# In-chunk products over all 128 rows with a zero-padded X, and a smaller descriptor ring for GpSimd

## The chip, the core and the metric

The kernel runs on one NeuronCore of a Trainium2 chip. Its engines are named as in the profile: PE (TensorE, the matrix engine; PEld is its loading of weights), DVE (VectorE), ACT (ScalarE), POOL (GpSimd) and SP (SyncE, which here only issues DMAs). The metric is device time in microseconds (us) of one execution.

## The reference

One layer of a flow-matching backbone is applied to 128 context tokens and 512 latent tokens, all of width 2048. Each layer is a mixer and a SwiGLU. The mixer splits one projection of the normed, modulated input into a bidirectional RWKV-7 scan (16 heads of 64) and a chunked gated MLP (8 groups of 128). The part that matters here is the scan, run forward and backward for each head:

```
def _delta_scan(r, w, k, v, aa, bb, s0, reverse):
    def step(S, inp):
        r_t, w_t, k_t, v_t, a_t, b_t = inp
        sa = jnp.einsum('bhvk,bhk->bhv', S, a_t)
        S = S * w_t[:, :, None, :] + sa[..., None] * b_t[:, :, None, :] + v_t[..., None] * k_t[:, :, None, :]
        return S, jnp.einsum('bhvk,bhk->bhv', S, r_t)
    s_fin, ys = lax.scan(step, s0, xs, reverse=reverse)

p = h @ lp['w_in']
o_a, s_fin = _rwkv7_bidir(shift_fn(p[..., :C_SHIFT], lp['mu_shift']), s0, lp)
o_b = _chunk_gmlp(jax.nn.gelu(p[..., C_SHIFT:]), lp)
x = x + g1 * (jnp.concatenate([o_a, o_b], axis=-1) @ lp['w_out'])
h = _rmsnorm(x, lp['norm2_g']) * (1.0 + sc2) + sh2
ff = (jax.nn.silu(h @ lp['w_ffn_gate']) * (h @ lp['w_ffn_up'])) @ lp['w_ffn_down']
```

All data are float32. Outputs are the two token streams after the last norm and the final context states of the scan.

## The kernel before, in words

Channels lie on the 128 partitions (rows) and the 640 tokens on the free axis, so a block of 128 channels holds a pair of heads: head 0 in rows 0 to 64, head 1 in rows 64 to 128. The kernel runs in five stages: modulation and norm (until about 190 us of the profile), the projection `w_in` with the preparation of the scan and the gated MLP (190 to 1200), the recurrence over chunks with half of `w_out` (to about 1560), the gate and up products, and the down product.

**The wide products of the second stage.** `win` (lines 179 to 189) multiplies blocks of `w_in` by the normed input. Both operands are split in a rounded part and a remainder (`hi`, `lo`), so a product of 128 rows by 320 tokens is made three times: lines 185, 186 and 187, tile `big`. These fill most of PE's time in this stage.

**The work between them.** Generators do everything else, and `Mixer.run` advances them a bit after some of the wide products (`between`, line 924), each `yield` carrying a planned cost. `take_r`, `take_v`, `take_k` prepare a pair of heads, `solve` (line 755) inverts 16 by 16 blocks on DVE, `merge` (line 783) puts them together to 64 by 64 ones with 32-row products on PE (lines 808, 834, 843). The framework then orders the instructions of each engine, finds the waits and places the tiles; each engine runs its own list in order.

**What the change touches, in `take_k`.** The scan is cut into 10 chunks (`NCH`) of 64 tokens (`CH`). For each of 8 pairs of heads and 2 directions `d`:

- GpSimd scales `tha` (line 601). DVE multiplies by it (602).
- DVE writes `X`, one tile per direction, with four products on 64 rows each (606, 607, 609, 610). For each chunk, `X` holds two blocks of 64 columns; in rows 0 to 64 (head 0) key first, in rows 64 to 128 (head 1) the other way round. `R` (582 to 590) holds the other operand of both heads, on 128 rows.
- Line 624 multiplies, chunk by chunk and head by head, 64 rows of `X` (the weights, 128 columns) by the same 64 rows of `R` (128 columns) into `two[h]`, a PSUM tile `pG` of four chunks: 8 x 2 x 10 x 2 = 320 products. `pG` has two buffers, which other tiles of tag `g` share.
- ACT and DVE take the results out (629, 631, 632); line 641 transposes `X`, line 652 makes a product over 64 rows with what line 632 left. Z, R and the results go to DRAM by SP's DMAs.
- GpSimd's own queue moves small blocks: `dd` (660), `mix` (761), `d2` (778), `TB` (788) and `TF` (848). [...]

GpSimd clears `A1_`, `TB` (752, 753) and `TF` (800) near the beginning.

Of the kernel before, what the change touches and what calls it, by code (L numbers as in the profile page):

```python
# [10 lines left out]
F32 = mybir.dt.float32  # L11
# [8 lines left out]
P = 128  # L20
# [5 lines left out]
CH = 64  # L26
NCH = T // CH
# [57 lines left out]
def flow_step(ctx: ExitStack, tc, x_prompt, x_sample, state_rwkv, c, c_ctx, w_mod, b_mod,  # L85
# [3 lines left out]
    nc = tc.nc  # L89
    V, S, G, TE = nc.vector, nc.scalar, nc.gpsimd, nc.tensor  # L90
# [19 lines left out]
    ident = cp.tile([P, P], F32, name="ident")  # L110
    make_identity(nc, ident)
    I2 = cb.tile([P, CH], F32, name="I2")
    for h in range(2):
        s = slice(CH * h, CH * h + CH)
# [86 lines left out]
    with ExitStack() as ph:  # L201
# [92 lines left out]
        def quarter(g, j):  # L294
# [17 lines left out]
            for cb in range(4):  # L312
                TE.transpose(pt[:, cb, :], ms[:, cb * P:(cb + 1) * P], ident)
            m = mc[:, g, 4 * j:4 * j + 4, :]
            V.tensor_reduce(out=m, in_=pt.rearrange("p cb (i r) -> p cb r i", r=32)[:, :, 0:2, :],
                            axis=AX.X, op=ALU.add)
            V.tensor_tensor(out=m, in0=m, in1=bc(bmod[:, g, 4 * j:4 * j + 4]), op=ALU.add)
# [34 lines left out]
    v3 = lambda ap: ap.rearrange("p (c t) -> p c t", t=CH)  # L352

    bk, bp, gs, bz = (hp.enter_context(tc.tile_pool(name=n, bufs=1)) for n in ("bk", "bp", "gs", "bz"))
    db = hp.enter_context(tc.tile_pool(name="db", bufs=2, space=DRAM))
    BQ = nc.gpsimd
    hsl = lambda h: slice(64 * h, 64 * h + 64)
# [139 lines left out]
            evac(ps, s)  # L497


    class Pair:  # L500
        pass

# [22 lines left out]
    def take_k(pr, p):  # L525
# [19 lines left out]
        for hf in range(2):  # L545
            s = slice(HALF * hf, HALF * hf + HALF)
# [5 lines left out]
        for d in range(2):  # L552
            rev = (lambda ap: ap[:, :, ::-1]) if d else (lambda ap: ap)
# [3 lines left out]
            tha = bp.tile([P, T], F32, tag="t3", name="tha", bufs=1)  # L557
            for hf in range(2):
                s = slice(HALF * hf, HALF * hf + HALF)
                two = [pk.tile([P, HALF], F32, tag="g", name="pwa") for _ in range(2)]  # L560
# [9 lines left out]
            for lo in (0, HALF):  # L570
                s = slice(lo, lo + HALF)
# [8 lines left out]
            n3, g3, i3 = v3(nkk), v3(gam), v3(L)  # L580
            R = bz.tile([P, NCH, 2, CH], F32, tag="R", name="R")
# [15 lines left out]
            f = fs if d == 0 else bk.tile([P, T], F32, tag="t1", name="f", bufs=2)  # L597
# [4 lines left out]
            V.tensor_mul(tha, tha, nkk)  # L602
            yield 0.8

            X = bz.tile([P, NCH, 2, CH], F32, tag="X", name="X", bufs=1)
            V.tensor_mul(rev(X[0:64, :, 1, :]), v3(tha)[0:64], i3[0:64])
            V.tensor_mul(rev(X[64:128, :, 0, :]), v3(tha)[64:128], i3[64:128])
            yield 1.5
            V.tensor_mul(rev(X[0:64, :, 0, :]), v3(f)[0:64], i3[0:64])
            V.tensor_mul(rev(X[64:128, :, 1, :]), v3(f)[64:128], i3[64:128])  # L610
            yield 1.5
            if d == 1:
                V.tensor_add(fs, fs, f)
# [5 lines left out]
            for (c0, c1) in ((0, 4), (4, 8), (8, NCH)):  # L619
                two = [pk.tile([P, 4, P], F32, tag="g", name="pG") for _ in range(2)]  # L620
                for cc in range(c0, c1):
                    for h in range(2):
                        s = hsl(h)
                        TE.matmul(two[h][:, cc - c0, :], X[s, cc, :, :].rearrange("p s t -> p (s t)"),
                                  R[s, cc, :, :].rearrange("p s t -> p (s t)"), start=True, stop=True)
                for h in range(2):
                    s, q, ps = hsl(h), osl(h), two[h]
                    mb = mask.unsqueeze(1).to_broadcast([P, c1 - c0, P])
                    S.copy(GB[q, c0:c1, :], ps[q, 0:c1 - c0, 0:CH])
                    GR = bk.tile([P, 4, CH], F32, tag="GR", name="GR", bufs=2)  # L630
                    V.tensor_tensor(out=GR[:, 0:c1 - c0, :], in0=ps[:, 0:c1 - c0, CH:P], in1=mb[:, :, CH:P], op=ALU.mult)
                    V.tensor_tensor(out=GA[s, c0:c1, :], in0=ps[s, 0:c1 - c0, 0:CH], in1=mb[s, :, 0:CH], op=ALU.mult)
                    yield 0.25 * (c1 - c0)
                    nc.sync.dma_start(d_S[p, :, d, c0:c1, F_G + CH * h:F_G + CH * h + CH], GR[:, 0:c1 - c0, :])

            for (c0, c1) in ((0, 8), (8, NCH)):
                two = [pk.tile([P, 8, CH], F32, tag="g", name="pXT") for _ in range(2)]
                for cc in range(c0, c1):
                    for h in range(2):
                        s = hsl(h)  # L640
                        TE.transpose(two[h][:, cc - c0, :], X[s, cc, :, :].rearrange("p s t -> p (s t)"), ident[s, s])
                for h in range(2):
                    ps = two[h]
                    XT = bz.tile([P, 8, CH], F32, tag="XT", name="XT", bufs=2)
                    S.copy(XT[:, 0:c1 - c0, :], ps[:, 0:c1 - c0, :])
                    yield 0.1 * (c1 - c0)
                    nc.sync.dma_start(d_S[p, :, d, c0:c1, F_X + CH * h:F_X + CH * h + CH], XT[:, 0:c1 - c0, :])
# [247 lines left out]
    for p in range(NPAIR):  # L895
        block(P * p, take_r, 2.6, p)
        block(2 * DA + P * p, take_v, 5.1, p)
        block(DA + P * p, take_k, KCOST, p)
        while g < GORD[p]:
            block(CSH + DA + P * g, take_gv, 12.0, g)  # L900
            block(CSH + P * g, take_gu, 5.0, g)
            g += 1
# [368 lines left out]
    X = {}  # L1271
# [61 lines left out]
    with ExitStack() as ph:  # L1333
# [21 lines left out]
        for hf in range(2):  # L1355
            s = slice(HALF * hf, HALF * hf + HALF)
# [502 lines left out]
    for t in range(NT):  # L1859
        for h in range(2):  # L1860
            out = fin.tile([P, 4, 256], F32, tag=f"out{h}", name="out")
            src, f = (ap[:, 4 * h:4 * h + 4] for ap in (acc[:, :, t * 256:(t + 1) * 256], fg))
# [36 lines left out]
```

## Time and profile before

| | |
|---|---|
| median of 3 runs | 3428.27 us (3420.05 to 3448.01) |
| the profiled execution | 3418.51 us, its span 3416.7 us |
| mean granted clock of PE | 0.973 |
| instructions | 72586 |
| line 624 | 640 matmul records, 93.46 us busy |
| read from and written to HBM | 436.68 MB, 111.28 MB |

The page of the profile lists the busy time of each engine; then the span in 40 slices, each digit a busy share in tenths, with a row PEclk for the clock that PE was granted; then the chain of work that ended last, followed back from the end. A group's row names the line, engine, operation, tile written and tiles read, then rows * columns of the weights and the shape that streams, and the count. A row of the timeline begins with its start and its length in us and ends, in brackets, with idle time before it and what ended that. The rows of windows give, for a stretch of time, its length, each engine's busy time with the number of instructions, the granted clock, the share of busy DMA engines and GB/s. Matmuls are pipelined and their recorded lengths overlap, so the start of one to the start of the next tells what it costs PE.

### The profile page before, as it was taken

Reading aid. Unit: us, or ns where it says so; the run is one execution under the profiler, and the core shown is the slowest. Engines: PE = TensorE matmul, PEld = TensorE weight load, DVE = VectorE, ACT = ScalarE, POOL = GpSimd, SP = SyncE. Lnnn points to the kernel's source line nnn. Section 1 sums busy time; section 2 is a strip of 40 time slices with the busy share of each in tenths; the row PEclk is TensorE's granted clock in tenths of the full one; section 3 lists DMA queues with packets and bytes.
Section 4 is the critical chain, followed back from the end, with each engine's and each line's share of the span. In section 5 each row is a group of like instructions: output and inputs, shape, how many; then the busy total and the mean of one; then the engine's idle time right before and its main releaser. Section 6 shows DMA issues by size and latency. Waiting matters only on the chain.

```text
span 3416.7 us, 72586 instructions
## 1 busy us (share of the span) xinstructions
PE 3253.2 (95%) x28260; PEld 2934.0 (86%) x28260; DVE 2413.6 (71%) x4320; ACT 1449.3 (42%) x3161; POOL 1239.6 (36%) x1090
## 2 busy tenths in 40 slices
PE   6899999999999999999899999999999999999996
PEld 3688777777877887768899999999999999999986
DVE  4547766765866666654887768777777777877787
ACT  3334444434444333323554444444444444443365
POOL 0001121112112103230136565656565655555543
PEclk8899999999999999999999999999999999999998
DMA  8766676766667587644533444343434354543453
GB/s 318 236 186 186 183 190 179 174 173 179 175 185 198 152 251 221 207 143 143 168 116 112 124 121 126 106 127 115 130 103 130 116 173 151 155 148 116 144 167 114
DMA packets 736176, 550.11 MB, mean 161 GB/s; under 512 B 140328, under 2 KB 670008, under 8 KB 727000
## 3 DMA queue, kind: packets, MB, share of 16 engines
q1 hardware_dynamic: 723512, 531.78, 52.3%
q0 software_dynamic: 9984, 13.13, 1.8%
q8 instruction: 222, 3.64, 0.4%
q14 instruction: 122, 1.00, 0.1%
q10 hardware_dynamic: 2336, 0.57, 0.1%
HBM read 436.68 MB, written 111.28 MB: 160 GB/s over the span
## 4 chain that ended last, share of the span: by engine, by line
PE 45%; DVE 4%; issue 4%; DMA 1%; POOL 0%; ACT 0%; DVEq 0%; SPq 0%; POOLq 0%; ACTq 0%
PE P L1513 14%; PE P L1511 14%; PE P L1512 14%; DVE lo L1330 1%; DMA opd<-d_op 1%; DVE xd L1564 1%; PE big L1366 0%; PE big L1364 0%; PE big L1365 0%; DVE xo L1291 0%; DVE out L1867 0%; PE C L1445 0%; PE C L1443 0%; PE C L1444 0%; POOL rawd L1424 0%
## 5 line engine op out<-in xcount | busy, mean ns | idle before, releaser
L1511 PE MATMUL P<-xo,hi 128*128 128x320 f32 x2352 | 727.7, 309 | 3.3 <-ACT hi L1329 3.3
L1513 PE MATMUL P<-xo,lo 128*128 128x320 f32 x2352 | 727.4, 309 | 1.9 <-DVE lo L1330 1.9
L1512 PE MATMUL P<-xo,hi 128*128 128x320 f32 x2352 | 727.4, 309 | 0.0
L1330 DVE TENSOR_TENSOR lo<-raw,hi 128x512 fp32r<-128x512 f32 x532 | 509.1, 960 | 177.1 <-ACT hi L1329 172.3
L1329 ACT CAST hi<-raw 128x512 fp32r<-128x512 f32 x532 | 330.7, 622 | 495.4 <-PE P L1512 399.1
L185 PE MATMUL big<-h_hi,hi 128*128 128x320 f32 x1376 | 456.3, 332 | 9.5 <-ACT hi L163 4.5
L1511 PEld LDWEIGHTS P<-xo,hi 128*128 128x128 f32 x2352 | 442.1, 188 | 3.5 <-ACT hi L1329 3.5
L1513 PEld LDWEIGHTS P<-xo,lo 128*128 128x128 f32 x2352 | 441.9, 188 | 2.3 <-DVE lo L1330 2.3
L187 PE MATMUL big<-h_hi,lo 128*128 128x320 f32 x1376 | 442.9, 322 | 0.7 <-DVE lo L164 0.7
L186 PE MATMUL big<-h_lo,hi 128*128 128x320 f32 x1376 | 441.8, 321 | 0.5 <-DVE h_lo L342 0.5
L1512 PEld LDWEIGHTS P<-xo,hi 128*128 128x128 f32 x2352 | 442.1, 188 | 0.0
L1424 POOL TENSOR_TENSOR raw<-raw 128x512 f32<-128x512 f32 x252 | 409.3, 1634 | 12.7 <-DVE lo L1330 1.1
L1513 PE MATMUL P<-xd,lo 128*128 128x320 f32 x1232 | 385.3, 313 | 17.6 <-DVE lo L1330 17.4
L1511 PE MATMUL P<-xd,hi 128*128 128x320 f32 x1232 | 383.2, 311 | 6.0 <-ACT hi L1329 2.6
L1512 PE MATMUL P<-xd,hi 128*128 128x320 f32 x1232 | 381.9, 310 | 0.0
L164 DVE TENSOR_TENSOR lo<-raw,hi 128x512 fp32r<-128x512 f32 x268 | 185.1, 693 | 247.9 <-ACT hi L163 225.0
L185 PEld LDWEIGHTS big<-h_hi,hi 128*128 128x128 f32 x1376 | 266.8, 194 | 83.3 <-issue 55.2
L163 ACT CAST hi<-raw 128x512 fp32r<-128x512 f32 x268 | 165.4, 619 | 302.5 <-PE big L186 142.6
L186 PEld LDWEIGHTS big<-h_lo,hi 128*128 128x128 f32 x1376 | 267.2, 194 | 17.9 <-issue 12.3
L187 PEld LDWEIGHTS big<-h_hi,lo 128*128 128x128 f32 x1376 | 266.8, 194 | 12.2 <-issue 4.8
L1329 ACT CAST hi<-rawd 128x512 fp32r<-128x512 f32 (+1 forms) x288 | 168.8, 587 | 239.0 <-PE P L1512 203.7
L1513 PEld LDWEIGHTS P<-xd,lo 128*128 128x128 f32 x1232 | 232.4, 189 | 25.5 <-DVE lo L1330 25.3
(358 smaller groups left out, 6288.3 us busy)
## 6 DMA issues: line engine op xcount, KB each, us to landing
wt<-in_w_mod_dram SPq DMA_DIRECT2D x96, 1024.0 KB
raw<-in_w_ffn_gate_dram SPq DMA_DIRECT2D x182, 256.0 KB
raw<-in_w_ffn_up_dram SPq DMA_DIRECT2D x182, 256.0 KB
rec<-d_S SPq DMA_DIRECT2D x80, 576.0 KB
raw<-in_w_in_dram SPq DMA_DIRECT2D x172, 256.0 KB
rawd<-in_w_ffn_down_dram SPq DMA_DIRECT2D x128, 256.0 KB
raw<-in_w_out_dram SPq DMA_DIRECT2D x96, 256.0 KB
xd<-d_os SPq DMA_DIRECT2D x66, 320.0 KB
```

The source lines that it names most:

```text
L163: S.copy(hi, raw)
L164: V.tensor_sub(lo, raw, hi.bitcast(F32))
L185: TE.matmul(halves[hf], hi[:, k, :], h_hi[:, kb, s], start=(kb == 0), stop=False)
L186: TE.matmul(halves[hf], hi[:, k, :], h_lo[:, kb, s], start=False, stop=False)
L187: TE.matmul(halves[hf], lo[:, k, :], h_hi[:, kb, s], start=False, stop=(kb == KB - 1))
L1329: S.copy(hi[:, 0:nk], raw[:, 0:nk])
L1330: V.tensor_sub(lo[:, 0:nk], raw[:, 0:nk], hi[:, 0:nk].bitcast(F32))
L1424: G.tensor_tensor(out=o[:, 0:nk], in0=p[:, 0:nk], in1=q[:, 0:nk], op=ALU.subtract)
L1511: TE.matmul(ps, hi[:, k, :], xk[:, 0, :], start=f, stop=False)
L1512: TE.matmul(ps, hi[:, k, :], xk[:, 1, :], start=False, stop=False)
L1513: TE.matmul(ps, lo[:, k, :], xk[:, 0, :], start=False, stop=l)
L1564: (G if (k + q) in POOLK else V).tensor_tensor(out=x[:, 1, :], in0=t[:, q, :], in1=x[:, 0, :].bitcast(F32), op=ALU.subtract)
```

## The change

`X` becomes `XZ`: one tile for the whole stage, with a block of all 128 rows for each head. The rows of the other head are zeros, cleared twice by GpSimd at the start (64 rows of 1280 elements each). The products of line 624 then read all 128 rows of both operands, the zeros taking the other head out. DVE's writes and the transposes of line 641 address the same 64 rows as before, in the new layout. `XZ` takes 10240 bytes of a partition where `X` took 5120; `dynamic_dma_scratch_size` is set to 4096, where no size was given before.

```diff
+    XZ = bz.tile([P, NCH, 2, 2, CH], F32, name="XZ")
+    for h in range(2):
+        G.memset(XZ[hsl(h), :, 1 - h], 0.0)
...
-            X = bz.tile([P, NCH, 2, CH], F32, tag="X", name="X", bufs=1)
-            V.tensor_mul(rev(X[0:64, :, 1, :]), v3(tha)[0:64], i3[0:64])
-            V.tensor_mul(rev(X[64:128, :, 0, :]), v3(tha)[64:128], i3[64:128])
+            V.tensor_mul(rev(XZ[0:64, :, 0, 1, :]), v3(tha)[0:64], i3[0:64])
+            V.tensor_mul(rev(XZ[64:128, :, 1, 0, :]), v3(tha)[64:128], i3[64:128])
             yield 1.5
-            V.tensor_mul(rev(X[0:64, :, 0, :]), v3(f)[0:64], i3[0:64])
-            V.tensor_mul(rev(X[64:128, :, 1, :]), v3(f)[64:128], i3[64:128])
+            V.tensor_mul(rev(XZ[0:64, :, 0, 0, :]), v3(f)[0:64], i3[0:64])
+            V.tensor_mul(rev(XZ[64:128, :, 1, 1, :]), v3(f)[64:128], i3[64:128])
...
-                        s = hsl(h)
-                        TE.matmul(two[h][:, cc - c0, :], X[s, cc, :, :].rearrange("p s t -> p (s t)"),
-                                  R[s, cc, :, :].rearrange("p s t -> p (s t)"), start=True, stop=True)
+                        TE.matmul(two[h][:, cc - c0, :], XZ[:, cc, h, :, :].rearrange("p s t -> p (s t)"),
+                                  R[:, cc, :, :].rearrange("p s t -> p (s t)"), start=True, stop=True)
...
-                        TE.transpose(two[h][:, cc - c0, :], X[s, cc, :, :].rearrange("p s t -> p (s t)"), ident[s, s])
+                        TE.transpose(two[h][:, cc - c0, :], XZ[s, cc, h, :, :].rearrange("p s t -> p (s t)"), ident[s, s])
...
-    nc = _bacc.Bacc("TRN2", target_bir_lowering=False, num_devices=1)
+    nc = _bacc.Bacc("TRN2", target_bir_lowering=False, num_devices=1, dynamic_dma_scratch_size=4096)
```

## The prediction

> **What bounds the kernel now.** I read the page first, then the busy time by stage.
>
> ```profile
> PE 3253.2 (95%) x28260; PEld 2934.0 (86%) x28260; DVE 2413.6 (71%) x4320; ACT 1449.3 (42%) x3161; POOL 1239.6 (36%) x1090
> PEclk8899999999999999999999999999999999999998
> PE 45%; DVE 4%; issue 4%; DMA 1%; POOL 0%; ACT 0%; DVEq 0%; SPq 0%; POOLq 0%; ACTq 0%
> ```
>
> ```profile
> core 0: us, PE busy (x) PEld busy (x) DVE busy (x) ACT busy (x) POOL busy (x), PEclk, DMA share, GB/s
> 190.00:1200.00 1010.00, 962.51 (x10586) 789.31 (x10585) 681.92 (x1352) 425.25 (x923) 192.08 (x305) 0.96 0.67 181
> ```
>
> PE is busy 95% of the span and no other engine holds more than 4% of the chain. The change lies in the stage from 190 to 1200 us, where PE is again busy 95%, DVE 68%, POOL 19%: what PE loses or gains there moves the end, unless a wait for DVE takes it up. The granted clock of that stage is 0.96.
>
> The edited line is L624:
>
> ```profile
> L624 PE MATMUL pG<-R,X x640: 272/272/579, 225.3 to 1085.2; 64*128 64x128 f32 x160
> DVE X L606: 15.9, 13
> ```
>
> There are 320 products in the code and 640 matmul records, two to a product. Before 13 of the groups PE sat idle for X (15.9 us in all): here DVE is late, not PE.
>
> **The change, part by part.**
>
> *Rows 64 to 128 in the product.* Starts in the timeline of PE show what a run of eight 64-row records (one head, four chunks) costs between the wide 128-row products:
>
> ```profile
> 612.70 0.30 PE L187 MATMUL big<-h_hi,lo 128*128 128x320 f32 x1
> 612.93 1.16 PE L624 MATMUL pG<-R,X 64*128 64x128 f32 x8
> 614.02 0.42 PE L185 MATMUL big<-h_hi,hi 128*128 128x320 f32 x1
> 614.28 0.31 PE L186 MATMUL big<-h_lo,hi 128*128 128x320 f32 x1
> 614.43 0.31 PE L187 MATMUL big<-h_hi,lo 128*128 128x320 f32 x1
> ```
>
> Wide products follow each other every 0.15 us (614.28 to 614.43), so without L624 the next would have started at 612.85 and its successor at 613.00; that successor started at 614.28. The run cost 1.28 us. The nearest row for the new form is L738, float32 too, 128 rows by 128 columns, in the same company:
>
> ```profile
> 305.11 0.31 PE L187 MATMUL big<-h_hi,lo 128*128 128x320 f32 x1
> 305.26 1.05 PE L738 MATMUL psp<-wspT,vt 128*128 128x128 f32 x8
> 306.07 0.39 PE L185 MATMUL big<-h_hi,hi 128*128 128x320 f32 x1
> 306.30 0.31 PE L186 MATMUL big<-h_lo,hi 128*128 128x320 f32 x1
> ```
>
> By the same count these eight cost 306.30 - 305.11 - 2 x 0.15 = 0.89 us, or 0.11 each, with no gap on either side. The difference, 0.39 us, is paid once for a run (0.08 before it, the rest behind), whatever its length, since one head's records follow each other every 0.11 us in both forms. Going through the timeline I count 31 runs of eight and 17 of four with no other kind among them, 15 of sixteen, and 11 others, mostly where the merge's 32-row products share the run; first and last:
>
> ```profile
> 260.99 1.13 PE L624 MATMUL pG<-R,X 64*128 64x128 f32 x8 [0.90 <-DVE X L606]
> 1079.14 1.16 PE L624 MATMUL pG<-R,X 64*128 64x128 f32 x8
> 272.75 0.71 PE L624 MATMUL pG<-R,X 64*128 64x128 f32 x4
> 988.72 0.71 PE L624 MATMUL pG<-R,X 64*128 64x128 f32 x4
> 225.32 2.01 PE L624 MATMUL pG<-R,X 64*128 64x128 f32 x16 [0.56 <-DVE X L609]
> 1075.57 2.41 PE L624 MATMUL pG<-R,X 64*128 64x128 f32 x16
> 681.82 1.16 PE L624 MATMUL pG<-R,X 64*128 64x128 f32 x16
> ```
>
> 48 one-head runs x 0.39 = 18.7 us gained. The runs of sixteen hold both heads. At their best (681.82) both ran beside each other, sixteen records in the 1.16 us that eight take alone; the new form needs 16 x 0.11 = 1.79, so 1.79 - 1.28 = 0.5 us is lost. At 225.32 the second head came late, and 2.01 + 0.2 against 1.79 is a gain of 0.4. Bounds for the 15: -6 to +7.5 us; I take 0, as most rows lie between. The 11 others: -4 (0.39 each) to +5.5 (0.5 each); I take 0.
>
> [...]
>
> *The granted clock.* All of the loss of clock in this stage comes in 12 spells at exactly half speed; first and last of them and the sum, then two pairs of neighbouring windows and three more spells:
>
> ```profile
> 263.19:270.02 6.83, 6.83 (x32) 4.11 (x34) 4.88 (x9) 1.31 (x4) 0.00 (x0) 0.50 0.39 85
> 1119.94:1123.35 3.41, 3.41 (x40) 3.35 (x32) 2.01 (x5) 2.01 (x4) 1.55 (x3) 0.50 0.33 73
> sum 81.94, PE 81.75 PEld 63.46 DVE 42.28 ACT 16.60 POOL 14.78; mean PE 6.81 PEld 5.29 DVE 3.52 ACT 1.38 POOL 1.23
> 386.07:389.49 3.42, 2.96 (x20) 2.56 (x21) 3.33 (x6) 0.44 (x2) 0.65 (x2) 1.00 1.07 296
> 389.49:392.90 3.41, 3.41 (x20) 3.08 (x21) 2.47 (x5) 0.29 (x1) 0.00 (x0) 0.50 0.84 263
> 689.86:693.27 3.41, 2.09 (x15) 1.82 (x13) 0.00 (x0) 0.62 (x1) 0.00 (x0) 1.00 0.68 209
> 693.27:696.69 3.42, 0.83 (x5) 0.74 (x6) 1.69 (x5) 0.11 (x1) 0.00 (x0) 1.00 0.16 38
> 939.03:942.45 3.42, 3.42 (x21) 3.09 (x20) 3.36 (x12) 0.00 (x0) 0.00 (x0) 0.50 0.43 94
> 444.10:457.75 13.65, 13.65 (x56) 12.32 (x55) 4.25 (x10) 1.90 (x5) 5.34 (x8) 0.50 0.74 160
> 805.91:819.57 13.66, 13.66 (x57) 10.91 (x56) 3.79 (x9) 1.74 (x5) 0.00 (x0) 0.50 0.56 148
> ```
>
> 82 us at half speed, up to 41 us lost. PE was busy 2.96 of 3.42 us before the fall at 389.49, 16 of its 20 matmuls being L624; with 2.09 us busy, all of it wide products, the clock stayed at 1.00 after 693.27. So idle time alone does not lower it: products on half the rows appear to count about half. That reading is mine; if right, full rows (of zeros or not) raise the count. The three spells that open behind windows full of L624 (263.19, 389.49, 939.03: 6.8 + 3.4 + 3.4 us) should not open; the two of 13.7 us (444.10, 805.91), behind windows in which PE mostly waited, should open but end after half their length, as L624 fills them. 27 us less at half speed is 13.7 us gained. Bounds: 0 (no effect of rows), and 32 us, if all eight spells near L624 go (the 82 us less the four without it, 17 us, halved).
>
> [...]
>
> *X in XZ.* The four writes a direction keep their count and shapes; DVE writes 64 rows of 640 elements with another stride between chunks, at 0.81 and 0.82 us:
>
> ```profile
> 1033.62 1.16 PE L624 MATMUL pG<-R,X 64*128 64x128 f32 x8 [1.11 <-DVE X L606]
> 1033.60 0.82 DVE L607 TENSOR_TENSOR X<-tha,L 64x640 f32<-64x640 f32 x1
> 1034.34 0.82 DVE L610 TENSOR_TENSOR X<-fs,L 64x640 f32<-64x640 f32 x1
> ```
>
> PE starts head 0 as its two writes end, before head 1's (L607, L610) run. In XZ, head 0's block is rows 0 to 64 from the same two writes and zeros from the memset, so nothing later is needed: 0, bound +1.65 us x 16 directions = 26 us if it waits for L607 and L610 after all. The transposes of L641 still take 64 rows: 0.
>
> *Memsets and ring.* POOL, from its timeline:
>
> ```profile
> 140.40 1.21 POOL L753 MEMSET TB<- 128x1280 f32 x1
> 217.59 1.09 POOL L601 TENSOR_SCALAR tha<-tha 128x640 f32<-128x640 f32 x1 [75.17 <-DVE fs L598]
> 321.38 5.25 POOL L788 DMA_DIRECT2D TB<-d  x8 [6.50 <-DMA d<-mx]
> 338.48 1.09 POOL L601 TENSOR_SCALAR tha<-tha 128x640 f32<-128x640 f32 x1 [11.85 <-DVE fs L598]
> ```
>
> Two memsets of 1280 elements on 64 rows, some 1.2 us each by L753's row, once, in POOL's 75 us of idle time before 217.59: 0. Without that cover they would delay X by 2.4 us once. The smaller ring matters if POOL has to wait for descriptors to drain; its densest burst is L788, eight DMAs in 5.25 us, behind which it idles 11.85 us before L601, on which X hangs. Up to that much stretch is free: 0, bound below.
>
> The sum: 18.7 + 0 + 0 + 13.7 = 32.4 us of PE time. A part vanishes into the waits for X, where DVE, not PE, sets the start; as most of the gain falls behind those waits, I keep 85%: 27 us. The profiled execution took 3418.5 us (span 3416.7 and 1.8 around it), 10 below the median of the runs, 3428.3, and below all three (3420.1 to 3448.0). From the one, 3391; from the other, 3401. I forecast 3398 us, the upper half, since a median of runs is asked.
>
> **The rivals.** With the same place between execution and median:
> - All eight spells near L624 go: (18.7 + 32) x 0.85 = 43 us, 3382. For it: each of the eight has L624 in or before it. Against: windows like 693.27 (PE busy 0.83 of 3.42) are idle whatever the rows.
> - The clock does not heed the rows: 18.7 x 0.85 = 16 us, 3409.
> - The waits for X take it all: 3425. Against: these waits sum to 15.9 us, less than the gain.
> - Slower: head 0 waits for head 1's writes, +26 us at L624, and the longer idle time holds the clock down, so that of the gains only 16 remain: +10 us, 3435. It decides from 1 us a direction (16/16). Against: the row at 1033.62 shows waits kept apart by what is written.
> - Slower: a ring that lets only one of L788's DMAs out at a time. The eight would take several times 5.25 us; past 5.25 + 11.85 = 17.1 us a burst, or 2.1 us a DMA, each us delays X. At 4 us a DMA it is 8 pairs x 15 us = 120 us, 3545. Nothing in the trace shows POOL waiting for room.
> [...]
>
> **How the numbers follow.** Forecast 0.32; all spells go 0.28; clock heedless 0.20; waits take it 0.07; head 0 waits 0.06; packing 0.04; ring 0.03. About 1% (34 us, so below 3394 or above 3462) is what a measurement of this kernel can tell from no change. Faster: the 0.28 and 0.06 of the forecast's lower edge, 0.34. Slower: the ring and half the packing case, whose price lies on the bound, with a rest for order changes, 0.07. Same: 0.59. The forecast's own range is 3380 to 3414. The wide range runs from 3370 (all runs and spells gained, nothing absorbed: 3428 - 51 - 7) to 3436 (head 0 waits).
>
> **What would show it.** L624 as 128*128 at one record every 0.11 us, wide products directly on it without the 0.39 us; in the stage from 190, a PEclk of 0.97 or 0.98, fewer windows at 0.50; unchanged L788 near 0.66 us a DMA; waits for X still on L606. It is wrong if L624's idle time moves to L607 or L610, if PEclk stays 0.96, or if PE's order differs so much that other stages move.

## The result, and the profile after

The kernel before took 3421.03 us on the chip of this comparison (median of 22 runs, 3407.41 to 3448.01), the changed one 3417.91 (22 runs, 3409.24 to 3428.39). (The 3428.27 in front of the prediction is the median of three runs.) The ratio is 0.9992, with a 95% interval of 0.998 to 1.0004: no difference that can be measured. The forecast was 3398. The profiled execution of the changed kernel took 3417.11 us, its span 3415.3. Lines of the changed kernel's code stand two to four lower: L624 is L626, the writes of X at L606 and L607 are L609 and L610, and L788 is L790.

The page after, the lines that answer to those of before:

```profile
PE 3235.9 (95%) x28260; PEld 2934.7 (86%) x28260; DVE 2411.4 (71%) x4320; ACT 1449.7 (42%) x3161; POOL 1246.3 (36%) x1092
...
PEclk8899999999999899999999999999999999999998
...
PE 45%; DVE 4%; issue 4%; DMA 1%; ACT 0%; POOL 0%; DVEq 0%; SPq 0%; ACTq 0%; POOLq 0%
```

PE is busy for 17 us less (3253.2 before), and yet the span is the same. One digit of the PEclk row has fallen to 8 where it was 9: the fourteenth slice, from 1110 to 1195 us. So the second stage first, then its end. The edited line in the changed kernel, from the groups of PE between 190 and 1200 us (busy, mean ns, idle before it):

```profile
L626 PE MATMUL pG<-R,XZ 128*128 128x128 f32 x640 | 91.3, 287 | 21.9 <-DVE XZ L609 16.1 <-DVE GA L634 4.0 <-DVE XZ L613 0.8
```

and its waits for X, from PE's waits between 190 and 1166 us (us in total, times, longest):

```profile
PE pG L626 <- DVE XZ L609: 16.1, 13, 2.2
...
PE pG L626 <- DVE XZ L613: 0.8, 1, 0.8
```

The idle time for X stays where it was, 13 times behind the first head's write (15.9 us before), and the second head's last write, L613, has the 0.8 us, once, that L610 had before. A run of eight, from PE's timeline after:

```profile
607.21 0.31 PE L187 MATMUL big<-h_hi,lo 128*128 128x320 f32 x1
607.36 1.05 PE L626 MATMUL pG<-R,XZ 128*128 128x128 f32 x8
608.17 0.39 PE L185 MATMUL big<-h_hi,hi 128*128 128x320 f32 x1
608.40 0.31 PE L186 MATMUL big<-h_lo,hi 128*128 128x320 f32 x1
```

By the prediction's count 608.40 - 607.21 - 0.30 = 0.89 us, where the old form took 1.28. The second stage ends earlier for it. Its last weight product and the first product of w_out behind it, from the rows of L185 and of L999 (L1001 after): count, ns, first to last start. Before, then after:

```profile
L185 PE MATMUL big<-h_hi,hi x1376: 303/308/637, 53.9 to 1190.1; 128*128 128x320 f32 x197
...
L999 PE MATMUL big<-oh,hi x256: 302/414/417, 1192.0 to 1515.9; 128*128 128x320 f32 x128
...
L1200 PE MATMUL pO<-I,Y x320: 218/218/367, 1294.1 to 1542.3; 64*64 64x64 f32 x160
```

```profile
L185 PE MATMUL big<-h_hi,hi x1376: 303/308/637, 53.9 to 1168.9; 128*128 128x320 f32 x197
...
L1001 PE MATMUL big<-oh,hi x256: 302/415/632, 1204.3 to 1514.4; 128*128 128x320 f32 x128
...
L1202 PE MATMUL pO<-I,Y x320: 218/218/367, 1292.6 to 1540.8; 64*64 64x64 f32 x160
```

Read the last column of L185: 1190.1 before, 1168.9 after. The second stage gained 21.2 us. Then the first product of w_out: 1.9 us behind it before, 35.4 us behind it after. At the first pO, in the recurrence that follows, 1.5 us of the 21 are left, and the span ends 1.4 us earlier. The gain came and was lost within the 124 us from 1169 to 1293. I call the time from the last weight product (L185) to the first pO the border: 104.0 us before, 123.7 after.

What is late there is a load. SP's timeline before (start, length):

```profile
1154.15 0.34 SPq L985 DMA_DIRECT2D ol<-d_o  x1
...
1155.02 0.50 SPq L985 DMA_DIRECT2D ol<-d_o  x1
...
1156.82 0.34 SPq L745 DMA_DIRECT2D d_o<-praw  x1
...
1158.23 0.92 SPq L985 DMA_DIRECT2D ol<-d_o  x2
```

and after:

```profile
1133.67 0.34 SPq L987 DMA_DIRECT2D ol<-d_o  x1
...
1136.35 0.34 SPq L747 DMA_DIRECT2D d_o<-praw  x1
...
1139.99 0.34 SPq L987 DMA_DIRECT2D ol<-d_o  x1
...
1172.59 0.33 SPq L747 DMA_DIRECT2D d_o<-praw  x1
...
1193.64 0.33 SPq L747 DMA_DIRECT2D d_o<-praw  x1
...
1195.88 1.94 SPq L987 DMA_DIRECT2D ol<-d_o  x4
```

The first w_out products need four pairs of oh and ol. One load (ol<-d_o) serves one pair. Before, all four are issued by 1159.2. After, the two early loads (1133.67, 1139.99) are those of the fifth and sixth pair, by the built program's list of SP's instructions; the first four pairs are the x4 at 1195.88. They stand in SP's queue behind the last gMLP block's output (d_o<-praw at 1193.64), for which SP waits 7.0 us on DVE. Meanwhile PE has nothing but transposes of x1T, each group waiting for its copy (5.4 us in 10 waits), and the small products of the recurrence. Stages of the border after (PE busy, PEld, DVE, ACT, POOL, granted clock, DMA share, GB/s):

```profile
1160.00:1180.00 20.00, 16.50 (x211) 13.86 (x200) 7.77 (x15) 8.65 (x21) 1.37 (x2) 0.87 0.57 189
1180.00:1200.00 20.00, 14.60 (x142) 11.42 (x144) 13.35 (x32) 5.66 (x20) 1.19 (x1) 0.50 0.71 236
1200.00:1220.00 20.00, 19.68 (x176) 17.81 (x173) 11.78 (x32) 7.03 (x23) 0.00 (x0) 0.78 0.67 206
...
1174.70:1208.83 34.13, 26.98 (x247) 20.89 (x245) 18.57 (x47) 12.52 (x43) 1.19 (x1) 0.50 0.79 260
```

The last row is one half-speed spell of 34 us. The kernel before has PE busy 19.25 to 20.00 of every 20 us between 1140 and 1300, all at clock 1.00. PE thus loses time twice in those 34.13 us: 7.15 in which it is idle, and 26.98 in which it works at half speed.

Why are they late? The addresses of the built program say it. The space that `dynamic_dma_scratch_size` sizes, the ring of the title, lies at address 0, below all tiles (what passes through it no run here shows); with 4096 instead of 16384 bytes the tiles of the second stage lie 12288 bytes lower in their partition (those in the pool of the larger XZ by less). The tiles of oh and ol are laid out from the other end and stay. The first four pairs occupy 126432 to 146912. Before, A1_ (151936) and TB (154496 to 159616), which the merge uses to the end of the second stage, lay above them. After, A1_ lies at 139648 and TB at 142208 to 147328, under the third and fourth pair. Theory P (placement): the loads cannot be ordered ahead of the merge's last use of A1_ and TB, and so they stand late in SP's queue. The queue then costs more than the merge: TB is last used at 1165.4, 30 us before the loads go out. Why the first and second pair, which lie under neither tile, are late as well is not shown; the four go close together in the kernels whose loads are given here. Rivals: Q, the third stage is bound by something else and takes whatever the second gives; R, the ring and not the rows shortened the second stage.

### The profile page after: what moved, and what is told of

The parts are those of the page before. It is cut to its first block, busy times and chain, and to the rows that moved or that the text cites. A ratio compares the mean times of both kernels' runs of the same rounds, so it can differ in the third digit from the quotient of the medians.

```text
span 3415.3 us, 72594 instructions
## 1 busy us (share of the span) xinstructions
PE 3235.9 (95%) x28260; PEld 2934.7 (86%) x28260; DVE 2411.4 (71%) x4320; ACT 1449.7 (42%) x3161; POOL 1246.3 (36%) x1092
## 4 chain that ended last, share of the span: by engine, by line
PE 45%; DVE 4%; issue 4%; DMA 1%; ACT 0%; POOL 0%; DVEq 0%; SPq 0%; ACTq 0%; POOLq 0%
PE P L1515 14%; PE P L1513 14%; PE P L1514 14%; DVE lo L1332 1%; DMA opd<-d_op 1%; DVE xd L1566 1%; PE big L1368 0%; PE big L1366 0%; PE big L1367 0%; DVE out L1869 0%; PE C L1447 0%; PE C L1445 0%; PE C L1446 0%; DVE xo L1293 0%; DVE cd L1751 0%
## 5 line engine op out<-in xcount | busy, mean ns | idle before, releaser
L185 PE MATMUL big<-h_hi,hi 128*128 128x320 f32 x1376 | 452.5, 329 | 7.3 <-ACT h_hi L341 3.7
L187 PE MATMUL big<-h_hi,lo 128*128 128x320 f32 x1376 | 438.6, 319 | 0.7 <-DVE lo L164 0.7
L185 PEld LDWEIGHTS big<-h_hi,hi 128*128 128x128 f32 x1376 | 264.1, 192 | 80.4 <-issue 54.2
L187 PEld LDWEIGHTS big<-h_hi,lo 128*128 128x128 f32 x1376 | 263.8, 192 | 9.8 <-issue 4.4
```

The lines of the kernel that those rows point to most:

```text
L185: TE.matmul(halves[hf], hi[:, k, :], h_hi[:, kb, s], start=(kb == 0), stop=False)
L187: TE.matmul(halves[hf], lo[:, k, :], h_hi[:, kb, s], start=False, stop=(kb == KB - 1))
```

## The experiments

Times in the expectations count from TensorE's first record, 8.8 us into the span: 1181 there is 1190 in the rows. Each ratio is to the kernel before on the same chip.

**e1, the ring alone.** In the kernel before: `num_devices=1, dynamic_dma_scratch_size=4096`.

> The kernel before with the smaller ring alone; the 64-row products stay. Theory P (placement): with the ring 12288 bytes of a partition smaller, the tiles of the second stage lie 12288 bytes lower, the third and fourth of the first four ol tiles come to lie over A1_ and TB, and their loads go out behind the last gMLP block's d_o<-praw. The last product big<-h_hi stays at 1181 us after the first TensorE record (before 1181.3, after the change 1160.3), the first product with oh comes some 20 us later than in the kernel before (near 1215 instead of 1183), and the time is 3435 to 3442 us (ratio 1.004 to 1.006). Rival Q (the third stage takes whatever the second gives): the late loads cost nothing that the third stage does not hide, the time is that of the kernel before, ratio 0.999 to 1.001. Rival R (the ring, not the rows, shortened the second stage): the last big<-h_hi comes near 1160 and the time is that of the changed kernel, 3418.

3438.52 us, ratio 1.0072 (1.0053 to 1.0092): slower. PE's order is that of the kernel before up to the last psp, and differs only behind it.

```profile
L185 PE MATMUL big<-h_hi,hi x1376: 303/308/636, 54.3 to 1190.6; 128*128 128x320 f32 x197
...
L999 PE MATMUL big<-oh,hi x256: 303/415/633, 1226.1 to 1536.4; 128*128 128x320 f32 x128
...
L1200 PE MATMUL pO<-I,Y x320: 218/218/363, 1314.5 to 1562.7; 64*64 64x64 f32 x160
```

```profile
1155.32 0.34 SPq L985 DMA_DIRECT2D ol<-d_o  x1
...
1161.40 0.45 SPq L985 DMA_DIRECT2D ol<-d_o  x1
...
1215.43 0.33 SPq L745 DMA_DIRECT2D d_o<-praw  x1
...
1217.66 1.75 SPq L985 DMA_DIRECT2D ol<-d_o  x4
```

The second stage ends at 1190.6 as before, the four loads go out at 1217.66 (the two early ones are again the fifth and sixth pair's), and the border takes 123.9 us, 20 more than the kernel before. Q and R fall: the ring alone costs 20 us at the border and gives nothing to the second stage.

**e2 to e4, three ways to get A1_ and TB out from under the loads**, all with the rows and the ring of the change. e2 adds an unused tile below the second stage's pools:

```
+    pad = bk.tile([P, 1824], F32, name="pad", bufs=1)
+    V.memset(pad[:, 0:1], 0.0)
     scan1 = bk.tile([P, HALF], BF16, name="scan1", bufs=1)
```

> The changed kernel with an unused tile of 7296 bytes at the bottom of the second stage's pools, so that A1_ begins at 146944, just above the first four pairs of oh and ol. Theory P: the four loads go out before the merge ends, the 21 us of the second stage reach the end: 3396 to 3402 us, ratio to the kernel before 0.993 to 0.9945, first product with oh within 5 us after the last big<-h_hi near 1160. Rival Q: the third stage is bound by something else, 3418, ratio 0.999.

e3 leaves the second stage alone and moves the loads:

```
-        o_hi[kb], o_lo[kb] = (obp[kb % 8 // 4].tile(
+        o_hi[kb], o_lo[kb] = (obp[1 - kb % 8 // 4].tile(
```

> The changed kernel with the two pools of oh and ol swapped: nothing moves in the second stage, only the first four pairs lie lower, under zr, zl, the raw of w_mod, zv and zk, which are done early. Theory P: 3396 to 3402 us, ratio 0.993 to 0.9945. Rival Q: 3418, ratio 0.999. A rival S (it is the second stage's own new placement, not the loads, that costs the time at the border) gives 3418 here too, but 3398 for the pad.

e4 moves A1_ and TB:

```
+    A1_ = bk.tile([P, 2, NCH, 32], F32, name="A1_", bufs=1)
+    TB = bk.tile([P, 2, NCH, 2, 32], F32, name="TB", bufs=1)
     XZ = bz.tile([P, NCH, 2, 2, CH], F32, name="XZ")
...
-    A1_ = bp.tile([P, 2, NCH, 32], F32, name="A1_")
-    TB = bp.tile([P, 2, NCH, 2, 32], F32, name="TB")
```

> The changed kernel with A1_ and TB at the front of the second stage's pools (from 99424 on), below the first four pairs of oh and ol. Theory P: 3396 to 3404 us, ratio 0.993 to 0.995; the four loads go out together once the last take_k has freed GA and GR, some 10 us later than in the kernel before but ahead of the end of the merge. Rival Q: 3418, ratio 0.999.

Ratios 0.9959 (0.9945 to 0.9973), 0.9955 (0.9939 to 0.997) and 0.9958 (0.9946 to 0.9971); medians 3399.93, 3399.48 and 3401.54 against 3416.74. All three gain 15 to 17 us, somewhat less than expected, and the borders are 104.5, 104.4 and 104.8 us long, as before. e3's rows:

```profile
L185 PE MATMUL big<-h_hi,hi x1376: 303/308/636, 55.5 to 1173.7; 128*128 128x320 f32 x197
...
L1001 PE MATMUL big<-oh,hi x256: 302/414/417, 1175.6 to 1499.9; 128*128 128x320 f32 x128
...
L1202 PE MATMUL pO<-I,Y x320: 218/218/366, 1278.1 to 1527.3; 64*64 64x64 f32 x160
```

Theory P holds: three edits that share only that A1_ and TB no longer lie under the first four pairs give the same. Rival S, named in e3's expectation, falls too, since e3 leaves the second stage's placement alone. In e4 the four loads go out together at 1170.78, later than I thought, and the border is as short: what matters is that they come ahead of the w_out products, not how far ahead.

**e5, the other half of the comparison**: the kernel before with the ring of 4096 and the pools swapped as in e3.

> The kernel before (64-row products) with the smaller ring and the pools of oh and ol swapped: the other half of the comparison with e3, which differs from this one only in the rows of the products. The order of every engine is that of the kernel before. If the smaller ring costs nothing by itself and the swap gains nothing by itself: ratio to the kernel before 0.999 to 1.001, and the rows' own worth is the 16 to 18 us that e3 lies lower. If the smaller ring slows GpSimd's DMAs where they matter: above 1.002. If the gain of e3 is the swap's own: 0.9955.

3421.14 us against 3420.27, ratio 1.0 (0.9985 to 1.0015). The ring costs nothing by itself where the order stays, and the swap gains nothing by itself. So the 0.45% of e3 is the worth of the rows, each measured against the kernel before on its own chip.

**e6, the transposes too.** e3 with

```
-                        TE.transpose(two[h][:, cc - c0, :], XZ[s, cc, h, :, :].rearrange("p s t -> p (s t)"), ident[s, s])
+                        TE.matmul(two[h][:, cc - c0, :], XZ[:, cc, h, :, :].rearrange("p s t -> p (s t)"), ident[:, s],
+                                  start=True, stop=True)
```

> e3 (changed kernel, pools swapped) with the 320 turned products pXT over all 128 rows as well, as a product with 64 columns of the identity. In the trace of the changed kernel 23 runs of two pXT cost 0.46 us each, 14 of eight 0.83, 8 of ten 0.71 and 4 of sixteen 1.08; at 0.055 us a record without the change of rows they would cost 0.11, 0.44, 0.55 and 0.88: 8 + 5.5 + 1.3 + 0.8 = 15.6 us. The rows of pG gave 28 us of TensorE's busy time and 16 to 21 of the stage. By the theory that a change of rows costs 0.39 us a run and that most of it reaches the stage's end: 3388 to 3395 us, ratio to the kernel before 0.991 to 0.9935. If the transposes' cost is hidden beside waits: 0.9955, as e3. Half-speed time before 1155 us, 48 us in e3, falls if products on half the rows count half.

3428.3 us, ratio 1.0021 (1.0009 to 1.0034): a miss, and mine. The group of the line in e3 and in e6:

```profile
L643 PE MATMUL pXT<-ident,XZ 64*128 64x64 f32 x320 | 29.8, 236 | 2.5 <-DVE GA L634 1.7 <-ACT XT L647 0.4 <-ACT vt L704 0.2
```

```profile
L643 PE MATMUL pXT<-ident,XZ 128*128 128x64 f32 x640 | 80.8, 278 | 2.3 <-ACT XT L648 1.2 <-DVE GA L634 0.8
```

In these rows a transpose is one record, a float32 product two: 640 instead of 320. Nor are they 0.055 us each: a run of two transposes (0.46 us) became four records of 0.45 us together, a run of eight (0.83) sixteen of 1.79. The change of rows was saved and paid for twice over: the second stage ends at 1198.1 instead of 1173.7. Half-speed time before 1155 us was 37.5 us where e3 had 47.8, but the other kernels with 128 rows in pG lie between 34.1 and 54.6, so this difference shows nothing by itself.

**e7, rows and clock by themselves.** Streams of float32 products with nothing beside them.

> No part of the reference is computed: eight streams of float32 products of 128 columns on TensorE alone, 800 each with 800 on 128 rows between them, then 100 groups of four on 64 rows and one on 128, then 60 groups of eight and two. By the price read from the trace: 128 rows 0.11 us a record, 64 rows of one head 0.11, two heads beside each other 0.055, a group of 4+1 0.94 us and one of 8+2 1.49 us (0.39 us for the change of rows included). By theory C (the clock counts active rows): the stream on 32 rows (weight 0.25) and the groups of 4+1 (weight 0.35) fall to the clock 0.50, the 128-row streams and the two heads beside each other stay at 1.00, and 64 rows alone (weight 0.5) lies near the bound and may go either way. By rival H (the clock counts streaming, whatever the rows): every stream without gaps stays at 1.00, 32 and 64 rows too, and the 4+1 groups (streaming 0.59 of the time) also. The stream with 32 of 128 output columns tells whether columns count.

Windows of it, one stream each (us, PE busy, PEld, DVE, POOL, granted clock, DMA share, GB/s), in order: 128 rows; 64 rows of one head; 32 rows up to the fall and behind it; 32 output columns; two heads beside each other; groups of 4+1; groups of 8+2:

```profile
0.00:186.00 186.00, 181.73 (x1601) 181.64 (x1602) 3.40 (x12) 0.74 (x7) 1.00 0.01 4
186.00:365.00 179.00, 179.00 (x1602) 178.88 (x1603) 0.00 (x0) 0.00 (x0) 1.00 0.00 1
...
543.40:549.30 5.90, 5.90 (x53) 5.78 (x53) 0.00 (x0) 0.00 (x0) 1.00 0.01 3
549.30:879.90 330.60, 330.60 (x1551) 330.45 (x1550) 0.00 (x0) 0.00 (x0) 0.50 0.00 1
...
1060.50:1235.30 174.80, 174.80 (x1602) 174.61 (x1601) 0.00 (x0) 0.00 (x0) 1.00 0.01 1
...
1414.20:1503.70 89.50, 89.50 (x1602) 89.41 (x1600) 0.00 (x0) 0.00 (x0) 1.00 0.01 2
...
1682.60:1832.80 150.20, 150.20 (x1001) 126.03 (x1000) 0.00 (x0) 0.00 (x0) 1.00 0.00 1
...
2011.60:2168.80 157.20, 157.20 (x1203) 142.74 (x1202) 0.00 (x0) 0.00 (x0) 1.00 0.00 1
```

800 products are 1600 records, so one costs 0.112 us on 128 rows and on 64, and 0.056 with the heads beside each other. I had taken a product for one record; counted rightly, a group of 4+1 is ten records and 1.50 us (150.2/100), ten times 0.112 and 0.38 for the change of rows, and its weight in rows 0.45 instead of 0.35. The clock: a stream on 32 rows, with PE busy all the time, falls to half speed 5.9 us after its start; rival H (streaming alone counts) is refuted. Weight 0.25 falls, 0.45 and 0.5 stay, and with 32 of 128 columns nothing happens. So rows count and columns don't, in this one run. If PE's time weighted by rows is what counts, the bound lies between the weights 0.25 and 0.45; 64 rows without gaps left it at 1.00 for 179 us.

**e8, e9: other sizes of the ring**, in the changed kernel: `dynamic_dma_scratch_size=8192`, then 11392.

> The changed kernel with a ring of 8192 bytes: every tile of the second stage 4096 bytes higher, A1_ at 143744 and TB at 146304, still under the last of the first four pairs (141792 to 146912). Theory P: no better than the changed kernel, ratio to the kernel before 0.998 to 1.001, with two ol loads early and the others behind the last d_o<-praw. If the size of the ring itself were at fault, half of the way back to 16384 would give part of it back: 0.997.

> The changed kernel with a ring of 11392 bytes, the smallest step at which A1_ (146944) clears the first four pairs (end 146912); with the larger XZ it just fits. Theory P: as the pad and the swapped pools, ratio to the kernel before 0.9945 to 0.997, 3400 to 3405 us. Rival: 0.999, as with 4096.

e9: 3404.73 against 3421.42, ratio 0.9938 (0.9913 to 0.9962), border 104.5 us. The smallest ring at which A1_ clears the four pairs brings the whole gain. e8: 3412.18 us, 0.9975 (0.996 to 0.9989), lower than expected, although its instructions have the order of the changed kernel on every engine and its loads are as late (1191.10, behind d_o<-praw at 1188.83). With 8192 bytes A1_ and TB reach under the fourth pair alone, and yet all four loads are late, not two as expected: one pair is enough. Its border takes 118.8 us, and its half-speed spell there is 17 us long instead of 34.

**e10, three PSUM banks for pG**, one for the merge, in e3 (`pk` with three buffers, `pt_` with one).

> e3 with three PSUM banks instead of two for the products inside the chunks (tag g) and one instead of two for the merge's (tag pt). In the changed kernel a run of eight pG costs 0.89 us at best but 1.00 to 1.15 in half of its cases, where its first record waits for the copy of the run before (ACT GB L631). If these waits for a bank are what takes the other half of the forecast: more runs at 0.89, the last big<-h_hi up to 5 us earlier than e3's 1164.5, ratio to e3 0.9985, unless the merge, with one bank, then waits by more, which would be seen as idle time of pblk, pM and pT. If the waits are for X from DVE and not for a bank: the second stage no shorter than e3's.

3402.99 us, 0.9941 (0.9918 to 0.9964); not to be told from e3. The second stage ends at 1171.7 (e3 1173.7). The waits moved: pG's for X fell from 15.5 to 10.5 us, and the weight products L185 and L187 now wait 5.7 and 4.5 us for hi and lo (0.6 and 0 in e3). PE then waits more for ACT and DVE, which split the weights.

**e11, e12: the changed kernel and e8 once more**, beside each other.

> The changed kernel as it is, on one chip beside e12. e8 has its instructions in the same order on every engine, and differs by the ring (8192 instead of 4096) and by all addresses 4096 higher alone; its trace had one half-speed spell of 17 us at the stage's border where that of the changed kernel had one of 34. Ratio to the kernel before 0.998 to 1.000, the spell 34 us again. If e8's 5 us are an accident of the chip or of the spell's length: a ratio equal to e12's within 0.001.

> e8 again beside e11. If the ring's size or the addresses have a worth of their own: 4 to 6 us less than e11 again and a short spell again. If not: the same as e11 within 0.001, and the length of the spell differs from profile to profile.

e11: 3415.43, 0.9994 (0.9978 to 1.001), border 123.3 us with 31 us at half speed in it. e12: 3411.29, 0.9979 (0.9964 to 0.9995), border 121.0 with 20.5. The spell was shorter with 8192 both times and the medians lie 4 us apart, but the intervals overlap. What makes the same order of instructions a little better there stays open; for e1's question it is enough that both are late.

## Why the prediction was wrong

**The step that failed**, and that took the gain, is the one on the ring: "Up to that much stretch is free: 0, bound below." It priced the ring by what POOL does with it, and there it was right: L790 takes 663 ns a DMA, where L788 took 664. But by the addresses of the built program the ring also lies ahead of the tiles: 16384 bytes of every partition before, 4096 after. Making it smaller moved A1_ and TB under the first tiles of the third stage, and the order of the loads followed. e1 prices it: 20 us at the border. The prediction named the sign of it under what would make it wrong ("PE's order differs so much that other stages move"), without a mechanism or a chance. Its rival "The waits for X take it all: 3425" has nearly the time that came out, but not its place: these waits did not grow.

**Rows, the price of a run**: right for one-head runs between wide products with no wait ahead of them. One-head runs of four between wide products went from 0.84 to 0.45 us in all 15 cases at full clock, runs of eight at best from 1.28 to 0.89, and e7 shows 0.38 in isolation. The chances hold 0.04 for a packing case, in which all heads run beside each other and the new form loses by it; no run shows that case. In e7 two heads beside each other take 0.056 us a record (89.50/1600) instead of 0.112; in this kernel 5 of the 54 places counted below hold both heads alone, they came out even, and the second stage got shorter.

**The clock**: right in size, and in kind as far as rows are concerned. Time at half speed in the second stage (190 to 1155 us) was 81.9, 75.1 and 64.9 us in the three kernels with 64 rows (before, e1, e5), 74 in the mean, and 34.1 to 54.6, in the mean 43.5, in eight traces with 128 rows and two banks (after, e2 to e4, e8, e9, e11, e12): 30 us less, where 27 were forecast. Other things count beside the rows: e10, with the same rows and three banks, has 23.9. The stage, up to 3 us ahead of its end, has the granted clock 0.96 before (first row) and 0.98 after:

```profile
190.00:1187.00 997.00, 950.12 (x10466) 777.99 (x10465) 677.57 (x1343) 419.83 (x910) 191.08 (x304) 0.96 0.67 180
...
190.00:1166.00 976.00, 922.30 (x10468) 768.76 (x10468) 675.31 (x1342) 418.20 (x908) 192.76 (x304) 0.98 0.68 183
```

The three spells that should not open (263.19, 389.49, 939.03) are gone in the trace after. Of the two of 13.7 us one is two spells of 3.4 (437.40 and 451.10), the other gone.

That rows count, and not idle time alone, can also be read in the kernel before. Here are two stretches of 3.41 us at full clock; in the traces before and after, the length of every spell between 190 and 1300 us is a multiple of that, from 3.41 to 34.13:

```profile
655.72:659.13 3.41, 2.81 (x163) 2.49 (x163) 3.33 (x7) 0.31 (x3) 0.00 (x0) 1.00 0.72 201
894.67:898.09 3.42, 1.58 (x12) 1.35 (x11) 3.30 (x7) 0.00 (x0) 0.00 (x0) 1.00 0.11 34
```

Behind the first, busy for 2.81 us but almost all of it with the merge's 32-row products, the clock falls (659.14). Behind the second, busy for 1.58 us with 128-row products alone, it stays. I weighted PE's time by rows over 128 in all such stretches between 190 and 1150 us of the thirteen traces with the whole kernel. This is an estimate from the starts and shapes of the records: 120 of the 122 falls come behind a weight under 0.42, and 67 of the 3335 stretches without a fall lie under it. By this estimate a product on half the rows counts about half, as the prediction read it.

By the rival in which the clock does not heed the rows this term would have been 0; e7's stream on 32 rows fell with PE busy for all of the 5.90 us before, so rows count beside idle time.

**The term of the rows** was mis-sized, and this is the second step that failed: 18.7 us were forecast, some 5 to 8 came. L624's products stand in 72 places between wide products. By the prediction's count, with idle time left out, the 54 places that lie at full clock in both traces (before, after) cost PE 7.9 us less after. The 15 runs of four gained 0.39 us each. The 13 runs of eight with no idle time ahead gained 0.30 in the mean; of the eight behind an idle PE seven gained only 0.18 to 0.20, where 0.39 was counted, and one lost 0.50. The 5 places with both heads alone came out even (0.2 gained). The 13 that L624 shares with other products lost 2.9 us together, where the prediction had counted 0 or 0.39 a run. One of them, in the trace after:

```profile
238.14 0.61 PE L626 MATMUL pG<-R,XZ 128*128 128x128 f32 x4
238.68 0.71 PE L643 MATMUL pXT<-ident,XZ 64*128 64x64 f32 x8
239.32 0.42 PE L185 MATMUL big<-h_hi,hi 128*128 128x320 f32 x1
```

Before, the same four records and eight transposes lay among each other, all on 64 rows, and the place cost 0.85 us; now the four run alone, the transposes still bring the change of rows, and it costs 1.28. In the 18 places with a half-speed spell in one of the two traces, counting half-speed time half, 3.2 us were lost, which leaves 4.6 in all.

One cause within the runs of eight can be read off: with the records faster, a run comes to its bank before the bank is empty. In the trace after:

```profile
262.60 0.37 ACT L631 COPY GB<-pG 64x256 f32<-64x256 f32 x1 [2.10 <-PE pG L626]
...
262.99 0.97 PEld L626 LDWEIGHTS pG<-R,XZ 128*128 128x128 f32 x8 [0.25 <-ACT GB L631]
...
263.02 1.13 PE L626 MATMUL pG<-R,XZ 128*128 128x128 f32 x8
```

The second run waits for the copy of the first. Twelve of the 26 one-head runs of eight at full clock cost 0.96 to 1.15 us instead of 0.89, 2.3 us in all.

**The account of the stage** then closes for these two traces: 23.9 us for the clock (half of 81.9 less 34.1) and 4.6 for the rows make 28.5, and PE's busy time from 190 us to 3 us ahead of the stage's end fell by 27.8 (950.12 to 922.30, in the rows of the windows above). Its idle time there grew from 46.9 to 53.7 us, which takes 6.8 back; the stage ended 21.2 us earlier. For e5 and e3 the same sums are 8.6 and 7.1 us, and 14.6 of busy time. In the pair before and after, the clock brought more than the 13.7 us forecast, and this hid the miss in the rows: that is luck. In the mean of the three kernels with 64 rows the stage ended at 1188.5, of the eight with 128 at 1170.8, 17.7 us earlier.

**X in XZ** and **the memsets**: 0 as forecast; L609 has the waits that L606 had, and the memsets of XZ (2.3 us) lie ahead of POOL's 75 us of idle time.

So the forecast's 27 us were some 17.7 in the second stage, with 20 lost at its border. With the placement mended, the same rows and a smaller ring give ratios of 0.9938 to 0.9959, 15 to 17 us below the kernel before by the medians: e2, e3, e4 and e9 beat both kernels, and e9 needs one number. That e2 to e4 lie near the forecast's 3398 us is luck: it was reckoned from a median that later runs put 7 us lower, and they gain 15 to 17 us where 27 were forecast.

## What to carry to other kernels

Here a smaller ring was also a change of addresses: by the built program the tiles of the second stage came to lie up to 12288 bytes lower, and that cost 20 us at the border (e1). So where the size of a buffer changes, look up which tiles of the next stage come to lie over the tiles that the last one holds longest, before pricing the rest. A gain within a stage is followed to the next stage's first products: here the loads at the border were late, 19.7 of the 21.2 us went there, and the clock went with it (one half-speed spell of 34 us). And where a change of rows is to be saved, count the records of the new form first (e6: 640 instead of 320), and look at what stands beside each run: here a neighbour on 64 rows (1.28 us for 0.85) or a wait ahead of the run (0.18 to 0.20 gained instead of 0.39) took the gain or half of it.

## What the runs showed of the hardware

In e7 TensorE's granted clock fell to 0.50 in a stream without any idle time, on 32 of 128 rows, 5.9 us after it began, and stayed there to the stream's end; over the 180.6 us of the 128-row stream that followed (879.90 to 1060.50 us) it was 0.99 in the mean. On 64 rows (179.0 us), on 128 rows with 32 columns (174.8) and on groups with a row weight of 0.45 (150.2) it stayed at 1.00. In the kernels the falls came behind stretches of 3.41 us with a row weight under some 0.42 (the estimate above: 120 of 122 falls in thirteen traces), whether PE was busy 2.81 us of them (655.72 in the kernel before) or 0.83 (693.27). In e7 a record on 32 rows took 0.213 us at half speed (330.6/1551) and 0.111 ahead of the fall (5.90/53). The same instructions in the same order, at other addresses, had half-speed spells of 34 and 31 us (the changed kernel, e11) or of 17 and 20.5 us (e8, e12) at the same place.
